# Fourier and attention encoder in fp32: Silu through Tanh, attention scores in two single banks, a one-tensor maxima step, p scaled on VectorE, and the weights' first piece first

## The chip, the cores and the metric

The kernel runs on one core of a Trainium2 chip. The metric is the device time of one execution in microseconds (us); the time before is the median of three runs. All products are fp32 values split into two fp32r parts (high and low), each product being three matmuls (high x high, high x low, low x high).

## The reference

Two sequences, a prompt of 1024 tokens and a sample of 512, go through the same two layers of width 1024. Layer 0 mixes by a Fourier transform, layer 1 by grouped-query attention (8 heads of 128, 2 key/value heads, RMS-normed and rotated q and k). A SwiGLU block of width 2816 follows each.

```python
def run_trunk(x):
    cos, sin = axial_rope_tables(x.shape[1])
    for i in range(DEPTH):                       # DEPTH = 2
        j = i // 2
        if i % 2 == 0:
            x = x + fourier_mixer(x, norm_mix[i], fourier_w[j])
        else:
            x = x + attention_mixer(x, norm_mix[i], attn_w_qkv[j], attn_q_norm[j],
                                    attn_k_norm[j], attn_w_o[j], cos, sin)
        x = x + swiglu_ffn(x, norm_ffn[i], ffn_w_gate[i], ffn_w_up[i], ffn_w_down[i])
    return x

# attention, per block of 128 queries
sc = jnp.einsum('bqkgd,bskd->bkgqs', qi, k).astype(jnp.float32) * scale
p = jax.nn.softmax(sc, axis=-1).astype(v.dtype)
return jnp.einsum('bkgqs,bskd->bqkgd', p, v)

# swiglu
h = rms_norm(x, g)
return (jax.nn.silu(h @ w_gate) * (h @ w_up)) @ w_down
```

## The kernel before

Tokens stand in three blocks of 512: block 0 is the sample, blocks 1 and 2 are the prompt. The program is a set of Python generators that emit instructions; a weaving loop lets two of them take turns by hand-given costs, F ("front": sample) and X ("aux": prompt), each with its own tiles (names that end in F or X) and PSUM banks. A scheduler then orders each engine's instructions by emission order and by when its own model takes them to be ready; an instruction that is `pinned` keeps its place among the pinned ones. On the chip each engine runs its list in order.

PSUM has 8 banks of 128x512 fp32. F has two of tag gF and two of cF, X two of cX and one pair of tag gX (`bank2`, one tile of two banks). `side` and `sides` give one or two working banks.

The order of the work: (1) the sample's Fourier mixer. `turned_weights` reads the folded Fourier weights in 8 pieces of 0.5 MB (`load`); `operand` forms their sum on VectorE (L648) and difference on GpSimd (L649) and splits them (ScalarE L651, GpSimd L652); `product` multiplies them with a DFT matrix; its last part needs `w64`, made from `stage` by `stacked`. `mixer` meanwhile folds the rows (`prepared`, L424 to L427), scales them and multiplies with the token DFT matrix `mat_s`; `mixer_projection` multiplies both. The functions `lead` and `follow` interleave the two. (2) The sample's first SwiGLU (`ffn`) woven with the prompt's Fourier mixer. (3) The prompt's first SwiGLU (`ffn_pair`, a Strassen-like scheme). (4) At its end the sample's q, k, v and attention (`attend` with one block, 32 chunks of 128 queries). (5) The prompt's q, k, v and attention (`attend` with two blocks, 64 chunks), woven with the sample's output projection and second SwiGLU. (6) The prompt's second SwiGLU.

In `attend`, for each chunk `scores` makes the 128 queries' scores against 512 or 1024 keys, takes the maximum of each half (L1371), joins them and scales by the negative factor of the row (L1372), takes Exp with the sum on the side (L1375), the sum's reciprocal (L1376), and multiplies p by it (L1377). `turned` transposes p on TensorE (L1389) and splits it (L242 on ScalarE, L243 on VectorE); `values` multiplies with v. The transposes of a chunk are emitted one chunk behind its scores.

In `ffn` each of 22 slices makes gate and up (24 matmuls each), scales gate by the row's factor (L851), takes Silu on ScalarE (L852), multiplies by the factor again on GpSimd (L853) and with up on VectorE (L854), and splits the result. `here` is true for the sample in layer 0.

Three lines use functions that need a table on ScalarE: L852, L1152 (Silu in `ffn_pair`) and L1375 (Exp). The table loads stand in the trace as ACT_TABLE_LOAD under these lines.

## Time and profile before

| | |
|---|---|
| time before, median of 3 runs | 2921.47 us (2921.27 to 2924.79) |
| the profiled execution | 2916.32 us, span 2914.5 us |
| granted TensorE clock, mean | 0.996 |
| busy share of the span | PE 97%, VectorE 59%, GpSimd 54%, ScalarE 45% |
| DMA moved | 490.53 MB, 168 GB/s on average |

Engines in the profile: PE is TensorE's matmuls and PEld its weight loads, which overlap; DVE is VectorE, ACT ScalarE, POOL GpSimd, SP the engine that issues most DMAs. A row of a group reads: line, engine, operation, out<-in, shapes, count | busy us, mean ns of one | idle time of the engine before them, and what ended it. A row of the timeline reads: start, length, engine, line, operation, names, [idle before it <- what ended that]. A row of the waits reads: who waited <- for whom: us in total, times, longest. A row of a source line gives min/median/max in ns, first and last start in us.

### The profile page before, as it was taken

The page shows a single profiled execution, that of the slowest core. Times are in us where ns is not written, and L with a number is a line of the kernel's source. Part 1 is how long each engine was busy: PE and PEld are TensorE (multiplying, and loading weights), DVE is VectorE, ACT ScalarE, POOL GpSimd, SP SyncE. Part 2 cuts the span into 40 slices and gives each one's busy share as a digit, 9 for nine tenths or more (in the row PEclk, how much of TensorE's full clock was granted, in tenths as well). Part 3 has the DMA queues.
Part 4 walks back from the last instruction along what each step waited for, and adds up shares of the span by engine and source line. Part 5 has one row for each costly group of instructions (what it writes and reads, how often), then busy time and mean ns, then how long its engine had stood idle before and what let it go on. Part 6 is the DMA issues. An engine that isn't in the chain of part 4 may idle for free.

```text
span 2914.5 us, 37209 instructions
## 1 busy us (share of the span) xinstructions
PE 2834.5 (97%) x13656; PEld 2341.5 (80%) x13656; DVE 1714.5 (59%) x3023; ACT 1304.7 (45%) x2134; POOL 1573.4 (54%) x976
## 2 busy tenths in 40 slices
PE   7999999999999999999999999999999999999999
PEld 6778878888888887787778888888888788888887
DVE  6664562466666666847656565553345466666666
ACT  6543242333333333646757776763333333333332
POOL 4445375767776676432332123224637667766774
PEclk9999999999999999999999999999999999999999
DMA  7435474766556653732332112115448865566553
GB/s 233 143 113 179 139 285 174 287 210 227 195 178 215 219 188 112 238 93 92 94 102 84 34 63 71 55 55 184 159 151 303 326 237 195 179 215 221 195 174 116
DMA packets 178870, 490.53 MB, mean 168 GB/s; under 512 B 19488, under 2 KB 29728, under 8 KB 177280
## 3 DMA queue, kind: packets, MB, share of 16 engines
q1 hardware_dynamic: 177760, 483.36, 48.7%
q0 software_dynamic: 640, 3.74, 0.4%
q8 instruction: 108, 1.77, 0.3%
q10 hardware_dynamic: 288, 1.05, 0.1%
q14 instruction: 74, 0.61, 0.1%
HBM read 422.01 MB, written 66.06 MB: 167 GB/s over the span
## 4 chain that ended last, share of the span: by engine, by line
PE 44%; DVE 3%; issue 2%; ACT 1%; DMA 1%; POOL 1%; SPq 0%; POOLq 0%; DVEq 0%; ACTq 0%
PE a L249 6%; PE a L251 6%; PE a L250 6%; PE c L249 5%; PE c L250 5%; PE c L251 5%; PE g L251 3%; PE g L249 3%; PE g L250 3%; PE c L1389 2%; DVE col L1372 1%; DVE col L1371 1%; DVE acc L1074 1%; POOL w L288 0%; ACT p L1375 0%
## 5 line engine op out<-in xcount | busy, mean ns | idle before, releaser
L288 POOL TENSOR_TENSOR w<-raw,w 128x1024 fp32r<-128x1024 f32 x200 | 479.6, 2404 | 762.3 <-ACT w L287 713.8
L243 POOL TENSOR_TENSOR w<-raw,w 128x512 fp32r<-128x512 f32 (+1 forms) x464 | 608.7, 1332 | 443.6 <-ACT w L242 431.6
L242 ACT CAST w<-raw 128x512 fp32r<-128x512 f32 (+1 forms) x464 | 279.5, 632 | 541.1 <-PE a L251 179.7
L287 ACT CAST w<-raw 128x1024 fp32r<-128x1024 f32 x200 | 209.4, 1049 | 275.2 <-PE g L251 94.5
L249 PE MATMUL g<-h,w 128*128 128x512 f32 x704 | 279.0, 396 | 3.5 <-DVE ss L339 2.0
L249 PE MATMUL a<-ring,w 128*128 128x512 f32 x708 | 277.4, 392 | 0.0
L251 PE MATMUL g<-h,w 128*128 128x512 f32 x704 | 276.2, 392 | 0.0
L250 PE MATMUL g<-h,w 128*128 128x512 f32 x704 | 276.1, 392 | 0.0
L251 PE MATMUL a<-ring,w 128*128 128x512 f32 x708 | 275.9, 390 | 0.0
L250 PE MATMUL a<-ring,w 128*128 128x512 f32 x708 | 275.7, 389 | 0.0
L1074 DVE TENSOR_TENSOR acc<-g,acc 128x512 f32<-128x512 f32 x294 | 201.8, 687 | 105.1 <-PE g L251 104.9
L1074 DVE TENSOR_TENSOR acc<-c,acc 128x512 f32<-128x512 f32 x294 | 201.7, 686 | 92.8 <-PE c L251 91.2
L249 PE MATMUL c<-mid,w 128*128 128x512 f32 x604 | 237.0, 392 | 7.0 <-DVE acc L780 4.9
L250 PE MATMUL c<-mid,w 128*128 128x512 f32 x604 | 236.4, 391 | 4.8 <-DVE mid L243 4.8
L251 PE MATMUL c<-mid,w 128*128 128x512 f32 x604 | 236.1, 391 | 0.0
L249 PE MATMUL c<-h,w 128*128 128x512 f32 x480 | 190.5, 398 | 2.1 <-ACT h L245 1.6
L250 PE MATMUL c<-h,w 128*128 128x512 f32 x480 | 188.7, 395 | 0.4 <-DVE h L246 0.2
L251 PE MATMUL c<-h,w 128*128 128x512 f32 x480 | 188.2, 393 | 0.0
L780 DVE TENSOR_TENSOR acc<-c,acc 128x512 f32<-128x512 f32 x176 | 121.0, 688 | 112.7 <-PE c L251 111.8
L249 PEld LDWEIGHTS a<-ring,w 128*128 128x128 f32 x708 | 133.0, 188 | 32.1 <-DVE mid L243 4.3
L249 PEld LDWEIGHTS g<-h,w 128*128 128x128 f32 x704 | 132.5, 188 | 30.1 <-DVE ss L339 2.2
L251 PEld LDWEIGHTS a<-ring,w 128*128 128x128 f32 x708 | 133.1, 188 | 27.9
(393 smaller groups left out, 6727.5 us busy)
## 6 DMA issues: line engine op xcount, KB each, us to landing
ring<-mov_B SPq DMA_DIRECT2D x248, 512.0 KB, 5.5
ring<-mov_T SPq DMA_DIRECT2D x88, 512.0 KB, 5.2
raw<-in_gate_dram SPq DMA_DIRECT2D x44, 512.0 KB, 3.6
raw<-in_up_dram SPq DMA_DIRECT2D x44, 512.0 KB, 3.5
raw<-in_down_dram SPq DMA_DIRECT2D x88, 256.0 KB, 3.0
raw<-in_gate_dram SPq DMA_DIRECT2D x88, 256.0 KB, 5.1
raw<-in_up_dram SPq DMA_DIRECT2D x88, 256.0 KB, 5.3
raw<-in_down_dram SPq DMA_DIRECT2D x44, 512.0 KB, 4.3
```

The source lines that it names most:

```text
L242: keep(act.copy(hi, src))
L243: keep(eng.tensor_tensor(lo, src, hi.bitcast(F32), op=ALU.subtract))
L249: pe.matmul(out, lh, rh, start=first, stop=False, **kw)
L250: pe.matmul(out, lh, rl, start=False, stop=False, **kw)
L251: pe.matmul(out, ll, rh, start=False, stop=last, **kw)
L287: pinned(act.copy(flat[:, 0], raw)) if early else act.copy(flat[:, 0], raw)
L288: pool.tensor_tensor(flat[:, 1], raw, flat[:, 0].bitcast(F32), op=ALU.subtract)
L780: dve.tensor_tensor(acc[dc], box[0], acc[dc], op=ALU.add)
L1074: dve.tensor_tensor(acc, chain[d], acc, op=ALU.add)
L1371: dve.tensor_reduce(st[:, 2 * kb : 2 * kb + 1], sc[:, kb], op=ALU.max, axis=AX.X)
L1372: dve.scalar_tensor_tensor(st[:, 1:2], st[:, 2 * nb - 2 : 2 * nb - 1], st[:, 0:1], nrqc[:, gq, h : h + 1], op0=ALU.max, op1=ALU.mult)
L1389: pe.transpose(tr[:, i * P : (i + 1) * P], p[:, kc * P : (kc + 1) * P], ident)
```

## The change

Six edits in one:

- `ffn` takes Tanh of half the gate instead of Silu, except for the sample in layer 0 (`here`): a new VectorE step forms (tanh + 1) x gate, and the missing half goes into the product with up.
- From the prompt's attention on, X has two single banks of tag gH in place of the pair gX: scores use one bank for each half, `side` and `sides` one each.
- Exp of the prompt's scores is taken in two halves of 512 with two sums, which VectorE adds; p is multiplied by the reciprocal on VectorE (`tensor_scalar`), in the sample still on ScalarE.
- The maxima step is a `tensor_scalar` with two per-partition scalars instead of a `scalar_tensor_tensor`.
- The statistics of a chunk (`st`, `sm`) both have 3 columns and so share one ring of four tiles.
- At the start the first weight piece is loaded ahead of the rows; piece 1, the mask, the stage rows, the token DFT matrix and its row come later; pieces are made one or two steps earlier in `lead`.

```diff
+        "gF": 2, "gX": 1, "gH": 2, "cF": 2, "cX": 2,
...
+    def single():
+        return tl("a", [TB], F32, "gH", pools["psX"])
+
     def side():
-        return bankg() if cur[0] == "F" else bank2()[:, 0]
+        return bankg() if cur[0] == "F" else single() if apart else bank2()[:, 0]
     def sides():
         if cur[0] == "F":
             return [bankg(), bankg()]
+        if apart:
+            return [single(), single()]
...
         load(0)
+        yield
         load(1)
         yield
...
-            act.activation(s, ga, AF.Silu)
+            if here:
+                act.activation(s, ga, AF.Silu)
+            else:
+                act.activation(s, ga, AF.Tanh, scale=0.5)
+                dve.scalar_tensor_tensor(s, s, 1.0, ga, op0=ALU.add, op1=ALU.mult)
             pool.tensor_tensor(s, s, first["r"], op=ALU.mult)
-            dve.tensor_tensor(up, up, s, op=ALU.mult)
+            if here:
+                dve.tensor_tensor(up, up, s, op=ALU.mult)
+            else:
+                dve.scalar_tensor_tensor(up, up, 0.5, s, op0=ALU.mult, op1=ALU.mult)
...
-                    sc = bankg().unsqueeze(1) if nb == 1 else bank2()
+                    sc = [bankg()] if nb == 1 else sides()
...
-                    dve.scalar_tensor_tensor(st[:, 1:2], st[:, 2 * nb - 2 : 2 * nb - 1], st[:, 0:1], nrqc[:, gq, h : h + 1], op0=ALU.max, op1=ALU.mult)
-                    sm = col(2)
+                    dve.tensor_scalar(st[:, 1:2], st[:, 2 * nb - 2 : 2 * nb - 1], st[:, 0:1], nrqc[:, gq, h : h + 1], op0=ALU.max, op1=ALU.mult)
+                    sm = col(3)
                     p = tmp(T) if nb == 1 else tl("p", [T], F32, "pX", ap)
-                    act.activation(p, s_in, AF.Exp, bias=st[:, 1:2], scale=rqc[:, gq, h : h + 1], accum_out=sm[:, 0:1])
+                    for kb in range(nb):
+                        act.activation(p[:, kb * TB : (kb + 1) * TB], sc[kb], AF.Exp, bias=st[:, 1:2], scale=rqc[:, gq, h : h + 1], accum_out=sm[:, 2 * kb : 2 * kb + 1])
+                    if nb == 2:
+                        dve.tensor_scalar(sm[:, 0:1], sm[:, 0:1], sm[:, 2:3], None, op0=ALU.add)
                     dve.reciprocal(sm[:, 1:2], sm[:, 0:1])
-                    act.activation(p, p, AF.Copy, scale=sm[:, 1:2])
+                    if nb == 1:
+                        act.activation(p, p, AF.Copy, scale=sm[:, 1:2])
+                    else:
+                        dve.tensor_scalar(p, p, sm[:, 1:2], None, op0=ALU.mult)
...
+    ws = turned_weights(w64, dd, odd, alt)
+    next(ws)
+    load_rows("s")
...
     def lead():
         next(ws)
+        sp.dma_start(mask, t["mask"])
+        next(ws)
+        pool.dma_start(m_s.rearrange("p c h n -> p (c h n)"), t["dft_s"])
         sp.dma_start(stage[0:96], t["wf64"])
+        row_in("s")
+        rows_of_dft("s")
         m = mixer("s", got_s, u_s, xrs_s, zz_s)
         for k, v in enumerate(m):
             yield v
-            if k == 3:
+            if k == 1:
                 stacked(w64[0:96], stage[0:96], 64)
-            if k < 3 or k % 2 == 0 and k < 14:
+            if k < 2 or k % 2 == 0 and k < 14:
                 next(ws)
...
     open_pool("psX", **RIGHT, **PS)
+    apart.append(True)
```

## The prediction

> **What bounds the kernel now.** I read the page first, then busy time by stage, then what TensorE waits for inside the stages that are not full, then the instructions ahead of those waits.

> ```profile
> span 2914.5 us, 37209 instructions
> PE 2834.5 (97%) x13656; PEld 2341.5 (80%) x13656; DVE 1714.5 (59%) x3023; ACT 1304.7 (45%) x2134; POOL 1573.4 (54%) x976
> ...
> 0.00:19.00 19.00, 14.24 (x87) 13.36 (x88) 8.47 (x15) 10.12 (x19) 6.73 (x13) 1.00 0.82 285
> 19.00:41.00 22.00, 11.62 (x35) 7.38 (x35) 18.97 (x36) 11.22 (x19) 12.75 (x7) 0.69 0.53 170
> 1340.00:1525.00 185.00, 173.41 (x947) 141.70 (x946) 114.02 (x263) 126.49 (x235) 55.38 (x29) 1.00 0.29 90
> 1525.00:1985.00 460.00, 441.17 (x2518) 372.51 (x2517) 277.93 (x507) 322.38 (x459) 130.51 (x60) 1.00 0.19 62
> ```

> The four stage rows give window, length, busy time of PE, PEld, DVE, ACT and POOL, granted clock, DMA share and GB/s. TensorE is the bound: it is busy 2834.5 of 2914.5 us, so 80 us are left. The change takes no matmul of the computation away, so it can only win idle time, and the changed lines touch three places that have some: the start (15.1 us idle to 41 us, part of what counts as busy there being the 72 warm-up matmuls), the sample's attention (1340 to 1525 us, 11.6 idle) and the prompt's (1525 to 1985 us, 18.8 idle).

> What TensorE waits for, first in the sample's window, then in the prompt's (sum, times, longest):

> ```profile
> PE c L1389 <- DVE h L243: 2.0, 3, 1.2
> PE c L249 <- ACT w L242: 1.5, 3, 1.2
> PE c L1389 <- ACT t L1377: 1.4, 1, 1.4
> PE g L249 <- ACT t L1375: 1.3, 2, 0.9
> ...
> PE a L249 <- ACT p L1375: 7.2, 7, 2.1
> PE c L1389 <- ACT p L1377: 5.0, 5, 1.5
> PE c L1389 <- ACT t L1403: 2.1, 2, 1.3
> PE c L1389 <- DVE h L243: 1.4, 1, 1.4
> ```

> These name the last link only. One chain in order of time shows where they begin:

> ```profile
> 1859.02 2.39 POOL L243 TENSOR_TENSOR w<-raw,w 128x1024 fp32r<-128x1024 f32 x1 [5.01 <-ACT w L242]
> 1859.22 2.21 DVE L1372 SCALAR_TENSOR_TENSOR col<-col,nrqc 128x1 f32<-128x1 f32 x1
> 1861.46 1.21 ACT L1375 ACTIVATE p<-a,col,rqc 128x1024 f32<-128x1024 f32 x1 [1.54 <-DVE col L1372]
> 1864.79 0.44 PE L1389 MATMUL c<-ident,p 128*128 128x128 f32 x2 [1.47 <-ACT p L1377]
> ...
> L1372 DVE SCALAR_TENSOR_TENSOR col<-col,nrqc x96: 199/218/2407, 1342.3 to 1976.3; 128x1 f32<-128x1 f32 x96
> L1372 DVE SCALAR_TENSOR_TENSOR col<-col,nrqc 128x1 f32<-128x1 f32 x64 | 41.8, 653 | 0.8
> ```

> A step on 128x1 numbers takes 0.22 us at the median but 2.41 at worst. Here it ends at 1861.43, when POOL's pass ends (1861.41), Exp waits 1.54 us for it, and 3.3 us on TensorE stands 1.47 us. The last row is the group in the prompt's window: 64 of them average 653 ns, so 28 us of VectorE time there are such waits.

> **The maxima step (L1372)** reads two SBUF tensors; it becomes a form with one tensor and two per-partition scalars. Whether that form also waits for POOL is shown by these:

> ```profile
> 26.45 1.59 POOL L649 TENSOR_TENSOR f<-raw 128x512 f32<-128x512 f32 x1
> 26.84 1.22 DVE L436 TENSOR_TENSOR m<-r_s,mask 128x1 f32<-128x1 f32 x1
> 28.13 2.60 POOL L652 TENSOR_TENSOR wm<-f,wm 128x1024 fp32r<-128x1024 f32 x1
> 28.45 0.13 DVE L437 TENSOR_SCALAR m<-m 128x1 f32<-128x1 f32 x1
> 1527.11 2.39 DVE L1323 TENSOR_SCALAR nrqc<-col 128x32 f32<-128x32 f32 x1
> ```

> The two-tensor 128x1 step waited for POOL's end at 28.04; the one-tensor 128x1 step took 0.13 us inside a POOL pass; the one-tensor step on 32 elements took 2.39 us. So the new form escapes at one element (one such row) and not at 32. [...]

> Sample's attention: its multiply stays on ScalarE, so here the wait simply goes. The four quoted rows hold 6.2 us; bounds 0 and 6.2. I take 4, as some of them have no long step ahead.

> **Prompt's scores in two single banks, p multiplied on VectorE.** For each of 64 chunks:

> ```profile
> L1375 ACT ACTIVATE p<-a,col,rqc 128x1024 f32<-128x1024 f32 x64 | 77.4, 1209 | 49.5 <-DVE col L1372 49.2
> L1377 ACT ACTIVATE p<-p,col 128x1024 f32<-128x1024 f32 x64 | 74.0, 1156 | 6.4 <-DVE col L1376 6.4
> L1375 ACT ACTIVATE t<-g,col,rqc 128x512 f32<-128x512 f32 x32 | 24.9, 779 | 17.2 <-DVE col L1372 17.2
> L1375 ACT ACTIVATION_READ_ACCUMULATOR p<-a,col,rqc 128x1 f32 x64 | 12.3, 192 | 0.0
> L1371 DVE TENSOR_REDUCE col<-a 128x1 f32<-128x512 f32 x128 | 82.9, 685 | 71.8 <-PE a L251 71.2
> L537 DVE TENSOR_SCALAR t<-x,r_s 1x512 f32<-1x512 f32 x1 | 0.5, 469 | 0.0
> L243 DVE TENSOR_TENSOR w<-a,w 128x1024 fp32r<-128x1024 f32 x4 | 4.9, 1220 | 1.4 <-ACT w L242 1.4
> ```

> ScalarE: two Exp of 779 + 192 replace one of 1209 + 192, +541 ns; the multiply's 1156 goes. Net -615, times 64 = -39 us. VectorE gains an add of two columns (0.13, L437's kind) and the multiply. A one-tensor step in SBUF takes 0.13 us at 1 and 0.469 at 512 elements, 0.66 ns an element, so 0.81 at 1024; bounds 0.47 (half the elements) and 1.22 (the two-tensor row of the same size). I take 0.80, the nearest form. [...]

> That multiply is over 32 elements, so it must wait for POOL as L1323 did. POOL is busy 130.5 of 460 us in this stage, 28%, mostly in 2.4 us passes: an estimate of 0.28 x 1.2 = 0.34 us a chunk against the 0.44 that L1372 loses now (653 less 210). So three quarters of the wait remains, but behind Exp rather than ahead of it. Bank release then no longer depends on it: the first bank is free after max, maxima step and one Exp, and the second maximum can follow its own matmuls alone. Of the 7.2 us of "a <- p L1375" I take 6 as gone. The other rows (5.0, 2.1, 1.4; 8.5 together) sit behind p or behind VectorE's queue, where the multiply now waits with the transposes' splits, the next maxima and FFN's accumulator adds queued behind it, and behind those TensorE for PSUM banks. The chain from the last score matmul to p gets shorter by 0.68 (first maximum beside the second half's matmuls), 0.36 (1.156 less 0.80) and 0.10 (0.44 less 0.34), longer by 0.54 (second Exp) and 0.13 (add): 0.47 shorter in all. Five waits of 1.0 on average, each 0.47 shorter, and the same share of the rest: I take 4 of 8.5. Together -10; bounds -16 (all 15.7 of the four rows) and, with VectorE overloaded, +17 (rival c). The statistics' tiles now share one ring of four instead of two rings: two chunks deep, and with one chunk of lag between scores and transposes the tile that is reused was last read a whole chunk (some 7 us, 460 over 64) before: nothing.

> **Silu by Tanh, layer 1 of the sample.**

> ```profile
> L852 ACT ACT_TABLE_LOAD x13 | 16.7, 1283 | 0.2
> L1375 ACT ACT_TABLE_LOAD x12 | 15.4, 1283 | 0.2
> L246 DVE SCALAR_TENSOR_TENSOR h<-a,gains,h 128x512 fp32r<-128x512 f32 x16 | 12.0, 747 | 5.1 <-ACT h L245 4.9
> 2256.18 1.29 POOL L853 TENSOR_TENSOR t<-t,ss 128x512 f32<-128x512 f32 x1
> 2259.10 0.70 DVE L854 TENSOR_TENSOR g<-g,t 128x512 f32<-128x512 f32 x1 [5.48 <-PE g L251]
> ```

> 22 times VectorE gets a 0.75 us step (L246's kind) between Tanh and POOL's product; the last product changes form at the same price within 0.05. Even where FFN runs alone POOL's product was done 1.6 us before "up" ended (2257.47 against 2259.10), and L854 waited for TensorE, so 0.75 is covered; without that cover it would be 22 x 0.75 = 16.5. The new step waits on VectorE for Tanh (some 0.78, the Exp row of that size), and what is queued behind it there waits too; in the prompt's stage that is 11 times and VectorE has 40% to spare. Of 25 table loads 22 go if Tanh needs none after Exp: 28.2 us of ScalarE's 322 in the prompt's stage and after. No row shows Tanh's table; the bounds are 0 and 28.2 of ScalarE time, and both are worth nothing by themselves, since ScalarE is 70% busy and the waits above begin at L1372. A later ffn_pair then loads Silu once, 1.28, beside matmuls. [...] FFN: 0.

> **Weights' first piece first.**

> ```profile
> 11.98 0.69 DVE L424 TENSOR_TENSOR x<-c,x 128x512 f32<-128x512 f32 x1 [2.03 <-DMA x<-in_rows_s_dram]
> 14.59 1.28 POOL L649 TENSOR_TENSOR f<-raw 128x512 f32<-128x512 f32 x1 [10.67 <-DMA raw<-in_wf_dram]
> 30.89 0.34 PEld L249 LDWEIGHTS c<-mat_s,comb 128*128 128x128 f32 x1
> ```

> On SP piece 0 goes ahead of the rows (one issue, some 0.6 us), piece 1, mask and stage after them; ScalarE's two row issues stay. On POOL the 1 MB DFT matrix and its row move behind the first piece's two passes (1.3 + 2.6), and so behind their waits for piece 0 and for ScalarE's split of it; the eo constants come first. DMA runs at 0.82 to 19 us, so order decides: 0.5 MB come before the rows, 1 MB after. The matrix is wanted at 30.9; from some 12 us on it has time. VectorE is the busiest to 41 us (18.97 of 22): it may lose the 2.03 us wait for rows and do piece 0's sum (0.7, a two-tensor step like L424) before them. Piece 2's sum and the split of the stage rows move ahead of the root that scales the rows and stood behind it: the same VectorE work in another order. Products of the weights go out earlier, which fills TensorE's cold stretch (clock 0.69), but the stretch ends when VectorE has the rows' units ready. So I take the two VectorE terms, 2.03 + 0.7, as -3; bounds -10 (piece 0 is first used at 14.59 now; if all follows it forward, at most the 10.4 us that TensorE idles from 19 to 41) and +2 (rows later by an issue and 0.5 MB at 285 GB/s).

> **Sum:** -4 - 10 - 3 = -17 on the profiled run's 2916.3 (span 2914.5 plus 1.8) is 2899.3. The median of the runs is 5.2 higher, so 2904.5.

> **Rivals.** (a) The wait only moves: VectorE's queue and p are as late as today and the prompt wins nothing: -4 - 3 = -7, 2914.5. For it: POOL's 2.4 us passes and L1323's 2.39; against: Exp and the banks no longer stand behind it. (b) One element waits too: then L1372 goes on as now, and the multiply waits besides. Nothing is won in the sample; in the prompt 3 of the 7.2, since a bank comes free 0.43 (1.209 less 0.779) sooner in each of seven waits; start -3: -6, 2915.5. [...] For it: the 32-element step; against: the 0.13 us row. (c) Slower: VectorE becomes the prompt's bound. Its 277.9 of 460 us take 64 x (1.22 + 0.34 + 0.14) = 109 and 11 x 0.75 = 8, less 28: 367, 80%, and each multiply holds back a split that frees a PSUM bank. If TensorE's waits there double (+17), -7 + 17 = +10, 2931.5; it decides from 13 us of new waits on, 0.2 a chunk. Against: at 0.80 the share is 74%.

> **Numbers.** Forecast 0.60, (a) 0.16, (b) 0.10, (c) 0.14. A change under 0.2%, 5.8 us, can't be told from none. (a) and (b) lie on that line, half of each on either side: faster 0.60 + 0.13, same 0.13, slower 0.14. The range goes from 2892 (-29, of the lower bounds' -6 - 15.7 - 10) to 2919 (-2: the start's +2 and a quarter of the 14 in the attentions), which takes in the forecast, (a) and (b) and leaves out (c) and the tails.

> **What would show it.** Right: L1372 at 0.2 us throughout; no "a <- Exp" wait over 0.5 us; the multiply 0.8 at the median and up to 3 us when POOL runs; no table loads from 1620 to 2015; POOL's first pass (L649) at about 7 us instead of 14.59. Wrong: L1372 still up to 2.4; TensorE waiting over 10 us for p after 1525; idle time to 41 us over 15.

## The result, and the profile after

The changed kernel takes 2902.41 us (median of four, 2899.95 to 2902.70) against 2921.37 us (2918.89 to 2924.79): a ratio of 0.9932, 95% interval 0.992 to 0.9945, so 19 us faster. One of the twelve runs of e2 below took 4723.8 us at a granted clock of 0.555 and is left out of e2's row. Lines have moved: the maxima step is L1384 (before L1372), Exp L1388 (L1375), the sum's add L1390 (new), the reciprocal L1391 (L1376), the prompt's multiply L1395 (on VectorE), the sample's L1393 (L1377, on ScalarE), the transposes L1407 (L1389); L243 and L249 to L251 are L248 and L254 to L256; L649, L302 and L424 are L655, L307 and L429.

The changed kernel's totals on the page, then its busy time by stage (columns as in the prediction):

```profile
span 2900.9 us, 37485 instructions
PE 2844.9 (98%) x13656; PEld 2348.8 (81%) x13656; DVE 1765.6 (61%) x3173; ACT 1226.6 (42%) x2176; POOL 1574.7 (54%) x976
```

```profile
0.00:19.00 19.00, 14.10 (x91) 12.74 (x91) 8.63 (x14) 10.57 (x20) 8.30 (x13) 1.00 0.90 302
19.00:41.00 22.00, 12.22 (x34) 7.62 (x35) 21.14 (x38) 13.79 (x24) 15.75 (x8) 0.84 0.56 168
1340.00:1525.00 185.00, 177.93 (x972) 146.87 (x971) 107.85 (x278) 128.01 (x239) 56.28 (x29) 0.99 0.30 95
1525.00:1985.00 460.00, 453.70 (x2585) 386.77 (x2584) 324.81 (x653) 249.69 (x507) 138.90 (x63) 1.00 0.22 71
```

TensorE's idle time fell from 11.6 to 7.1 us in the sample's attention and from 18.8 to 6.3 us in the prompt's, 17 us together. To 41 us it stayed: 15.1 before, 14.7 now.

What TensorE waits for in the prompt's window now (sum, times, longest); before, this list began with 7.2 us for Exp's bank:

```profile
PE c L1407 <- DVE p L1395: 3.2, 4, 1.6
PE a L256 <- POOL w L248: 1.7, 1, 1.7
PE c L254 <- DVE pt L248: 1.0, 1, 1.0
PE c L1407 <- DVE pt L248: 0.3, 1, 0.3
```

The changed instructions, by line (durations in ns: least, median, most), and then their groups in the prompt's window and all that is left of the table loads:

```profile
L1384 DVE TENSOR_SCALAR col<-col,nrqc x96: 253/272/277, 1348.1 to 1964.7; 128x1 f32<-128x1 f32 x96
L1395 DVE TENSOR_SCALAR p<-p,col x64: 742/753/2843, 1535.5 to 1967.5; 128x1024 f32<-128x1024 f32 x64
```

```profile
L1395 DVE TENSOR_SCALAR p<-p,col 128x1024 f32<-128x1024 f32 x64 | 50.7, 792 | 1.6
L1390 DVE TENSOR_SCALAR col<-col 128x1 f32<-128x1 f32 x64 | 13.6, 213 | 50.4 <-ACT p L1388 50.2
L862 DVE SCALAR_TENSOR_TENSOR t<-t,g 128x512 f32<-128x512 f32 x11 | 7.5, 682 | 1.2 <-ACT t L861 1.1
```

```profile
L225 ACT ACT_TABLE_LOAD x1 | 1.3, 1283 | 1.2 <-PEq L1719 1.2
L859 ACT ACT_TABLE_LOAD x1 | 1.3, 1283 | 0.0
L1388 ACT ACT_TABLE_LOAD x1 | 1.3, 1283 | 0.0
L1165 ACT ACT_TABLE_LOAD x1 | 1.3, 1283 | 0.0
```

The maxima step never waits now: 96 times, at most 277 ns, where 2407 was seen before. 33 of the 96 lie wholly inside a pass on POOL. Of the two-tensor steps before none does: 31 took over 300 ns, and each of them ended 11 to 23 ns behind an instruction of POOL. The multiply costs 0.75 us, and 0.79 with its waits. Each of the four loads left is the only one of its line, so the 22 Tanh (L861) between the Exps took none.

### The profile page after: what moved, and what is told of

Its sections match the earlier page's. It is cut to its first block, busy times and chain, and to the rows that moved or that the text cites. A ratio compares the mean times of both kernels' runs of the same rounds, so it can differ in the third digit from the quotient of the medians.

```text
span 2900.9 us, 37485 instructions
## 1 busy us (share of the span) xinstructions
PE 2844.9 (98%) x13656; PEld 2348.8 (81%) x13656; DVE 1765.6 (61%) x3173; ACT 1226.6 (42%) x2176; POOL 1574.7 (54%) x976
## 4 chain that ended last, share of the span: by engine, by line
PE 85%; DVE 6%; ACT 2%; issue 2%; DMA 2%; POOL 2%; SPq 0%; ACTq 0%; POOLq 0%; DVEq 0%
PE a L254 11%; PE a L256 11%; PE a L255 11%; PE c L254 10%; PE c L255 9%; PE c L256 9%; PE g L254 7%; PE g L256 7%; PE g L255 7%; PE c L1407 2%; POOL w L293 1%; DMA raw<-in_up_dram 1%; DVE acc L1087 1%; PE c L1272 1%; ACT w L292 1%
## 5 line engine op out<-in xcount | busy, mean ns | idle before, releaser
L248 POOL TENSOR_TENSOR w<-raw,w 128x512 fp32r<-128x512 f32 (+1 forms) x464 | 608.1, 1331 | 432.7 <-ACT w L247 409.6
L254 PE MATMUL g<-h,w 128*128 128x512 f32 x704 | 280.1, 398 | 3.5 <-DVE ss L344 1.8
L254 PE MATMUL a<-ring,w 128*128 128x512 f32 x708 | 277.3, 392 | 0.0
L256 PE MATMUL g<-h,w 128*128 128x512 f32 x704 | 277.1, 394 | 0.0
L256 PE MATMUL a<-ring,w 128*128 128x512 f32 x708 | 276.0, 390 | 0.0
L254 PE MATMUL c<-mid,w 128*128 128x512 f32 x604 | 237.2, 393 | 4.7 <-DVE acc L786 2.4
L256 PE MATMUL c<-mid,w 128*128 128x512 f32 x604 | 235.9, 391 | 0.0
L254 PE MATMUL c<-h,w 128*128 128x512 f32 x480 | 192.1, 402 | 2.0 <-ACT h L250 1.6
L256 PE MATMUL c<-h,w 128*128 128x512 f32 x480 | 190.4, 398 | 0.0
L254 PEld LDWEIGHTS a<-ring,w 128*128 128x128 f32 x708 | 132.9, 188 | 32.1 <-DVE mid L248 4.3
L254 PEld LDWEIGHTS g<-h,w 128*128 128x128 f32 x704 | 132.9, 189 | 30.3 <-DVE ss L344 2.0
L256 PEld LDWEIGHTS a<-ring,w 128*128 128x128 f32 x708 | 132.9, 188 | 28.0
```

The source lines that it names most:

```text
L248: keep(eng.tensor_tensor(lo, src, hi.bitcast(F32), op=ALU.subtract))
L254: pe.matmul(out, lh, rh, start=first, stop=False, **kw)
L256: pe.matmul(out, ll, rh, start=False, stop=last, **kw)
```

## The experiments

All times, each with the ratio to runs of the kernel before on the same chip. Kernels of a block were run together; a ratio can be compared across blocks, a median only roughly.

| kernel | us | ratio | 95% interval |
|---|---|---|---|
| changed kernel | 2902.4 | 0.9932 | 0.9920 to 0.9945 |
| e1: changed, old start | 2901.1 | 0.9941 | 0.9925 to 0.9956 |
| e2: before + new start | 2922.2 | 1.0009 | 0.9997 to 1.0020 |
| e3: before + one-tensor step | 2893.6 | 0.9913 | 0.9896 to 0.9929 |
| e4: changed, two-tensor step | 2921.6 | 1.0010 | 1.0000 to 1.0020 |
| e5: changed, p on ScalarE | 2897.6 | 0.9921 | 0.9907 to 0.9936 |
| e6: changed, pair of banks | 2906.7 | 0.9947 | 0.9932 to 0.9962 |
| e7: changed, Silu | 2905.4 | 0.9945 | 0.9931 to 0.9958 |
| e8: e3 without the two-column ring | 2907.4 | 0.9954 | 0.9941 to 0.9968 |
| f1: changed + 128 unused bytes | 2894.2 | 0.9912 | 0.9895 to 0.9929 |
| f2: e5 + 128 unused bytes | 2890.2 | 0.9899 | 0.9879 to 0.9918 |
| f3: e3 + 128 unused bytes | 2901.6 | 0.9943 | 0.9926 to 0.9960 |
| f4: e3 + 256 unused bytes | 2894.7 | 0.9912 | 0.9894 to 0.9931 |

### First block: which part carries the gain

**e3, the step alone** in the kernel before:

```
- dve.scalar_tensor_tensor(st[:, 1:2], st[:, 2*nb-2 : 2*nb-1], st[:, 0:1], nrqc[...], op0=ALU.max, op1=ALU.mult)
+ dve.tensor_scalar(st[:, 1:2], st[:, 2*nb-2 : 2*nb-1], st[:, 0:1], nrqc[...], op0=ALU.max, op1=ALU.mult)
```

> The kernel before with the one-tensor maxima step alone; banks, Exp, p's multiply on ScalarE and Silu as before. Theory 'wait for POOL': the step's 40 us of waits vanish (0.2 us at the median, none over 0.5) and with them most of TensorE's waits behind them, 5 in the sample's attention and 10 to 14 of 16 in the prompt's: 2921.4 - 15 to -19 = 2902 to 2906, as much as the whole change. Theory 'chain and banks': the step is a small part, -4 to -6, 2916, and the rest comes from the halves, the banks and ScalarE's load.

One line gives 0.9913, about 25 us, more than the whole change and more than the 15 to 19 us of the theory. Its step, the prompt's stage, and all that TensorE still waits for there, from three views:

```profile
L1372 DVE TENSOR_SCALAR col<-col,nrqc x96: 255/266/276, 1342.8 to 1952.1; 128x1 f32<-128x1 f32 x96
```

```profile
1525.00:1985.00 460.00, 459.11 (x2626) 391.52 (x2625) 253.48 (x506) 327.01 (x467) 137.66 (x63) 1.00 0.22 75
```

```profile
PE c L249 <- DVE pt L243: 0.5, 1, 0.5
PE c L1389 <- ACT p L1377: 0.2, 1, 0.2
```

TensorE idles 0.9 of 460 us, against 18.8 before and 6.3 in the whole change. The waits for banks ("a <- p") are gone and those for p ("c <- p") fell from 5.0 to 0.2 us, although banks, Exp and the multiply are as before: they began at this step.

**e4, all but the step**: the line above turned back in the changed kernel.

> The changed kernel with the old two-tensor maxima step. 'Wait for POOL': the step waits again in about a third of its 96 runs, up to 2.4 us, ahead of Exp, and the time goes up by 10 to 16, to 2912 to 2918. 'Chain and banks': the shorter chain and the single banks cover most of it, +3 to +5, 2906.

1.0010, slower than either theory had it: without the step, the rest wins nothing (a cost that was found later, that of the addresses, is inside this number). TensorE's idle time in the prompt's stage is 15.6 us, against 18.8 before. The longest of the prompt's waits of e4 show where the time stays:

```profile
PE c L254 <- DVE pt L248: 4.6, 7, 1.1
PE a L254 <- ACT p L1388: 2.8, 3, 1.7
PE a L256 <- POOL w L248: 2.5, 1, 2.5
PE c L1407 <- DVE pt L248: 2.1, 3, 1.6
PE c L1407 <- DVE col L1384: 1.5, 1, 1.5
```

The bank's wait fell from 7.2 to 2.8 us, as single banks were to bring. By these rows, what stands behind the stalled step on VectorE (the transposes' splits, pt) became late in its place; no run takes the two apart.

**e1 and e2, the start**: undone in the changed kernel (e1), and done alone in the kernel before (e2; shortened here, e1 is the reverse).

```
- load_rows("s"); pool.dma_start(m_s, t["dft_s"]); row_in("s"); sp.dma_start(mask, ...)
+ next(ws)                       # the weights' first piece
+ load_rows("s")
+ ... next(ws); sp.dma_start(mask, ...); next(ws); pool.dma_start(m_s, t["dft_s"]) ...
```

> The changed kernel with the start in its old order; everything from the sample's first SwiGLU on as changed. Theory 'start costs': the new start puts TensorE at the same place by 90 us as the old one and then meets a stretch of half clock from 92.4 us on for 10.2 us, so without it the time is some 3.5 us shorter than the changed kernel's 2902.4, 2899, and the trace shows no half clock between 41 and 130 us. Theory 'start gains', as predicted: 3 us longer, 2905.5. If the half clock at 92 us is chance of one execution, within 1 us of 2902.4.

> The kernel before with the new start alone. 'Start costs': 3.5 us longer than before's 2921.4, 2925, with half clock near 92 us. 'Start gains': 2918.4. The root that scales the sample's rows ends near 32 us instead of 25.4 by either, since this was seen in the changed kernel.

1.0009 alone and 0.9941 against 0.9932 when undone: nothing that can be measured, in either direction. The half-clock stretch on which the theory of a cost rested (10.2 us from 92.4 us on) is in e2's profile too, and e1 has one of 3.4 us at 83.4 us, yet neither time shows a cost. The order of time (start in us, duration) shows why. Of the kernel before, the prediction has POOL's first pass at 14.59 and the first load from mat_s at 30.89; the rows' first step on VectorE and their root, of the same kernel, are:

```profile
8.67 1.29 DVE L424 TENSOR_TENSOR x<-c,x 128x512 f32<-128x512 f32 x2 [7.67 <-DMA x<-in_rows_s_dram]
...
25.44 0.16 DVE L302 SCALAR_TENSOR_TENSOR r_s<-c,col 128x4 f32<-128x4 f32 x1
```

The same four in the changed kernel:

```profile
8.82 1.77 POOL L655 TENSOR_TENSOR f<-raw 128x512 f32<-128x512 f32 x1 [5.98 <-DMA raw<-in_wf_dram]
...
11.22 1.92 DVE L429 TENSOR_TENSOR x<-c,x 128x512 f32<-128x512 f32 x3 [1.76 <-DMA x<-in_rows_s_dram]
...
32.38 0.15 DVE L307 SCALAR_TENSOR_TENSOR r_s<-c,col 128x4 f32<-128x4 f32 x1
...
36.60 0.29 PEld L254 LDWEIGHTS c<-mat_s,comb 128*128 128x128 f32 x1 [0.37 <-ACT comb L247]
```

The weights come 5.8 us earlier, and the rows pay for it: their first step is 2.6 us later, the root 6.9, the first DFT product 5.7. The two orders trade one wait for the other.

### Second block: what takes a part of the step's gain back

The whole change holds the step and is still 9 us above e3 by the medians (0.9932 against 0.9913). Four suspects, each by itself.

**e5, p multiplied on ScalarE again**:

```
- if nb == 1: act.activation(p, p, AF.Copy, scale=sm[:, 1:2])
- else:       dve.tensor_scalar(p, p, sm[:, 1:2], None, op0=ALU.mult)
+ act.activation(p, p, AF.Copy, scale=sm[:, 1:2])
```

> The changed kernel with one edit undone: the prompt's p is multiplied by the sum's reciprocal on ScalarE again, as the kernel before does. The changed kernel alone is 2902.4 us; the maxima step alone gives 2893.6. Theory: the multiply on VectorE is what takes back a part of the step's gain (64 x 0.79 us more on VectorE in 1525-1985 us, and TensorE's waits for p on VectorE, 3.2 us in four); without it the time falls by about 5 us, to some 2897, and the waits of the transposes for p on VectorE are gone. Rival, the prediction's: the multiply unloads ScalarE and helps or costs nothing; then 2902 to 2906, with waits for p on ScalarE in their place.

2897.6 us, near the theory's 2897, though the intervals of e5 and of the changed kernel overlap. Its prompt's waits:

```profile
PE a L254 <- ACT p L1388: 1.7, 1, 1.7
PE a L256 <- POOL w L248: 1.4, 1, 1.4
PE c L1404 <- DVE pt L248: 0.5, 1, 0.5
PE c L1404 <- ACT p L1392: 0.5, 1, 0.5
```

The wait for p is 0.5 us in place of 3.2, while one wait for a bank, 1.7, is new. TensorE's idle time in the stage is 4.2 us in place of 6.3.

**e6, the pair of banks and one Exp of 1024**:

```
- for kb in range(nb): act.activation(p[...], sc[kb], AF.Exp, ..., accum_out=sm[:, 2*kb : 2*kb+1])
- if nb == 2: dve.tensor_scalar(sm[:, 0:1], sm[:, 0:1], sm[:, 2:3], None, op0=ALU.add)
+ act.activation(p, s_in, AF.Exp, ..., accum_out=sm[:, 0:1])       # s_in: both banks
```

> The changed kernel with one edit undone: the prompt's scores go into the pair of banks again and one Exp reads all 1024 columns, in place of two single banks and two Exps with an add of their sums; p stays on VectorE. Theory: with the step no longer waiting, the halves are an extra 64 Exps' fixed cost and an extra add for each chunk and nothing else; without them the time falls by about 3 us, to some 2899. Rival, the prediction's: the single banks come free earlier and are worth a part of the 10 us of the prompt's stage; then the waits of the scores for a bank that Exp reads return, 3 to 5 us, and the time is about 2906.

2906.7, the rival's number; the theory that the halves cost 3 us falls. That the single banks win anything is not shown: the intervals of e6 and of the changed kernel overlap. The bank's wait comes back, smaller than the 7.2 us of before, now that the step no longer stalls:

```profile
PE a L254 <- ACT p L1389: 2.6, 3, 2.2
PE a L256 <- POOL w L248: 1.7, 1, 1.7
```

The wait for p shrinks beside it (0.3 us, from 3.2), and TensorE's idle time in the stage is 5.8 us, against 6.3 in the changed kernel.

**e7, Silu**: the Tanh, its VectorE step and the 0.5 of the last product go, `act.activation(s, ga, AF.Silu)` returns.

> The changed kernel with Silu as its own function again in place of Tanh and VectorE's step for it. Theory: 22 table loads of 1.28 us return on ScalarE and VectorE loses its steps of 0.68 us for them; both stand beside TensorE's matmuls, so the time stays within 1 us of 2902.4. Rivals: the loads stand in the way of an Exp or of a Silu that TensorE waits for, then +2 us or more; or VectorE's step is what costs in the SwiGLU stages, then -2 us, and the matmuls' mean spacing in 700-1000 us falls from 228.6 to 227.7 ns.

2905.4: 3 us above the changed kernel, and intervals that overlap. TensorE idles 8.9 us in the prompt's stage in place of 6.3. Tanh is worth 0 to 3 us; that its VectorE step costs in the other stages is ruled out, as e7's matmuls still follow each other at 228.6 ns in the mean (the next experiments show what that hangs on).

**e8, the addresses alone**, e3 with `sm = col(3)` for `sm = col(2)`. The changed kernel takes the sums from the ring of three-column tiles. The ring of two-column tiles, four of 32 bytes a partition, then no longer exists, and every tile laid out behind it lies 128 bytes lower. Tiles laid out from the other end, such as op, stay.

> The kernel before with the one-tensor maxima step (2893.6 us by itself) and one more edit: the sum's column is taken from the ring of three-column tiles, as the changed kernel takes it, so that the ring of two-column tiles is gone and the tiles allocated after it lie at other addresses. No instruction is added or moved. Theory: the changed kernel's slower matmuls in the SwiGLU stages (mean spacing 228.6 against 227.7 ns in 700-1000 us) come from these addresses; then the spacing is 228.6 here too and the time is about 4 us longer, 2897.5. Rival: they come from something else that the change does; then the spacing is 227.7 ns and the time within 1 us of 2893.6.

0.9954 against e3's 0.9913, with not one instruction added: some 12 us, three times what the theory asked for. This is the cost that no part of the prediction had.

### Third block: the addresses

```
+ cols.tile([P, 32], F32, tag="pad", name="pad", bufs=1)     # 128 bytes; 256 in f4; never used
```

> The changed kernel (2902.4 us) with 128 unused bytes a partition allocated in the pool of columns, so that the tiles behind it lie at the addresses of the kernel before. No instruction differs. Theory: the lost ring of two-column tiles is the whole of what takes the step's gain back (0.41% between the step alone with and without the ring), so the time falls by 10 to 14 us, to 2889 to 2893, and the matmuls' mean spacing in 700-1000 us is 227.7 ns again. Rival: only the spacing's part, some 7 us, comes back, and the rest between the two kernels was the clock at the start; then about 2896. Second rival: the addresses matter only together with the old order of work; then 2901 to 2904.

> The kernel before with the one-tensor maxima step (0.9913 of before) and 128 unused bytes a partition, so that the tiles behind it lie 128 bytes higher. No instruction differs. Theory: what counts is where these tiles lie modulo 256 bytes against those that are laid out from the other end, which do not move; then 128 up is as bad as 128 down: 0.995 of before, spacing 228.6 ns. Rival: moving them down did harm by something particular to those addresses; then 0.9913 and 227.7 ns.

> The same with 256 bytes. Theory (modulo 256): as the kernel with the step alone, 0.9913 of before, spacing 227.7 ns. Rival: any other place than the old one costs, 0.995 and 228.6 ns.

f1 got 8 us back by the medians and 6 by the ratios, a little under the theory's 10 to 14 and between it and the first rival; the second rival falls. It stands where e3 stands (0.9912 and 0.9913): at the old addresses the other five edits together win and lose nothing that these intervals, 5 us to either side, could show. In the profiles they take and give: TensorE idles 6.7 us in f1's prompt's stage and 0.9 in e3's, but 0.6 and 5.0 from 1985 to 2400 us. f3 and f4 differ as their theory had it. The stage from 500 to 1000 us, where TensorE is full in all kernels and the work is the same; rows in the order e3, e8, the changed kernel, f1, f3, f4:

```profile
500.00:1000.00 500.00, 499.00 (x2196) 409.90 (x2195) 307.90 (x481) 180.08 (x321) 354.95 (x246) 1.00 0.62 213
```

```profile
500.00:1000.00 500.00, 498.99 (x2188) 408.35 (x2187) 306.81 (x478) 180.33 (x321) 354.01 (x245) 1.00 0.62 211
```

```profile
500.00:1000.00 500.00, 499.02 (x2188) 408.43 (x2187) 306.25 (x479) 181.10 (x323) 354.35 (x245) 1.00 0.62 212
```

```profile
500.00:1000.00 500.00, 499.01 (x2196) 409.90 (x2195) 306.77 (x479) 181.55 (x323) 355.61 (x247) 1.00 0.61 212
```

```profile
500.00:1000.00 500.00, 498.96 (x2188) 408.34 (x2187) 305.67 (x477) 179.56 (x320) 354.13 (x245) 1.00 0.61 210
```

```profile
500.00:1000.00 500.00, 498.97 (x2195) 409.86 (x2194) 306.97 (x480) 180.00 (x321) 356.63 (x247) 1.00 0.62 213
```

With the tiles at the old place (e3, f1) or 256 bytes up (f4), 2195 or 2196 matmuls start in 500 us; 128 bytes down (e8, the changed kernel) or up (f3), 2188. TensorE is as busy and waits for next to nothing in both (1 us of 500); each matmul is 0.36% slower on average. The distance from one start to the next tells how: from 700 to 1000 us its mean is 227.7 to 227.8 ns in the one group and 228.6 to 228.7 in the other, the median 227 in both, the 95th percentile 227 to 229 in the one and 235 in the other. About one in ten takes 5 to 8 ns more. The groups that read op, from 700 to 1000 us, are among them (e3, then e8):

```profile
L251 PE MATMUL a<-op,w 128*128 128x512 f32 x40 | 15.6, 389 | 0.0
```

```profile
L251 PE MATMUL a<-op,w 128*128 128x512 f32 x40 | 15.8, 394 | 0.0
```

So the place modulo 256 bytes fits all four places that were tried, and both rivals of f3 and f4 fall. Four pairs price it: 0.41% (e8 to e3), 0.31% (f3 to f4), 0.20% (changed to f1) and 0.22% (e5 to f2), 6 to 12 us. That two blocks of tiles must agree, and not the one block by itself, fits that op did not move and its matmuls became slower. The addresses that the built kernels give their tiles bear it out, with the starts of the same matmuls compared one by one (those of 512 columns, 222 to 246 ns apart). In e3 and f1 the streamed operand and the weights that are loaded for the next matmul lie in the same half of a 256-byte step in all but one of these cases. In e8 they lie in different halves in 1540 cases, and there the distance to the next start is 4.3 ns longer than in e3 in the mean; in the 8157 others it is 0.5 longer. In the changed kernel against f1 it is 4.1 ns (1578 cases) and 0.5 (8204).

**f2, the best version**: e5 with the 128 bytes.

> The same 128 bytes in the changed kernel whose prompt's p is multiplied on ScalarE (0.9921 of before, about 5 us better than the changed kernel). Theory: the two gains add, as they lie in different things (waits for p, addresses): 5 us below the padded changed kernel, some 2885 to 2888, the best version. Rival: with the matmuls at full rate the waits for p fall elsewhere and the multiply's place is worth nothing; then within 2 us of the padded changed kernel.

0.9899, 2890.2 us, the lowest of all, 2 us above what was expected. The multiply's place is worth 0.13% beside f1, as it was 0.11% without the bytes: two pairs that agree, each inside its own interval.

## Why the prediction was right, and where its steps were not

The forecast was 2904.5 and the time is 2902.4. The sum came out for the mechanism that it named first, but its terms share the gain out wrongly, and that the total is so near is in part luck: costs that it did not have and gains that it did not have nearly cancel (the last two paragraphs of this section).

**The step: right.** One element with one tensor does not wait for POOL, in 192 cases of two kernels (253 to 277 ns), 65 of them wholly inside a POOL pass. Rival (b), by which one element waits too, fell with it.

**The sample's -4: right** (11.6 less 7.1 is 4.5 us of idle time).

**The prompt's -10: size near, cause wrong.** 12.5 us of idle time went. The prediction gave that to the single banks and the shorter chain, and left the step only what lay ahead of Exp. The failed step is "three quarters of the wait remains, but behind Exp rather than ahead of it". It took the multiply to meet a POOL pass as often as chance would have it, 0.34 us a chunk. Measured: a mean of 792 ns against a median of 753, 0.04 a chunk; three of 64 waited, the longest for the 2843 ns in the row of L1395 above. In eight other cases POOL's pass began 0.11 to 0.54 us behind the multiply's start and took 2.46 to 2.90 us, against 2.40; this is one of them:

```profile
1741.99 0.76 DVE L1395 TENSOR_SCALAR p<-p,col 128x1024 f32<-128x1024 f32 x1
1742.10 2.90 POOL L248 TENSOR_TENSOR w<-raw,w 128x1024 fp32r<-128x1024 f32 x1 [1.04 <-ACT w L247]
```

With the stall gone at its root, e3 shows that nothing was left in this stage for the other edits to win: idle time 0.9 us. Without it, the other edits take the 18.8 us only to 15.6 (e4). So the gain here belongs to the step.

**Rival (c), VectorE as the bound: false as a bound, true in small.** VectorE is busy 324.8 of 460 us, 71%, near the 74% worked out. Still TensorE waits 3.2 us for p on VectorE, and moving the multiply there seems to lose 3 to 5 us (e5, f2; each pair inside its interval), where the prediction had it shorten the chain. Its 0.80 us was right (0.75); the queue on VectorE was priced too low, behind accumulator adds and splits of 0.68 each. **Rival (a)** fell: the waits did not move, they went.

**Tanh's 0: right** within what can be told (0 to 3 us), with the 22 table loads gone and 0.68 us for the new VectorE step where 0.75 was taken.

**The start's -3: wrong.** It measured nothing. The step that failed is "the same VectorE work in another order", together with taking two VectorE terms as saved: the order put the weights' steps ahead of the root, and root and first DFT product came 6.9 and 5.7 us later. The sign named for it, POOL's pass at about 7 us, came nearly (8.8), and was no sign of a gain. The bound that was named for harm, an issue and 0.5 MB on the rows' way, was the right place: the rows' first step came 2.6 us later.

**Two things it did not have.** The shared ring was priced "nothing", by the reuse of its tiles; what it did was to move addresses, +6 to +12 us. And a gap of the kernel before outside the changed stages is gone:

```profile
2264.09 1.08 DVE L1035 TENSOR_TENSOR s<-raw,raw 128x512 f32<-128x512 f32 x1 [4.29 <-DMA raw<-in_gate_dram]
2265.10 0.68 DVE L243 TENSOR_TENSOR mid<-g,mid 128x512 fp32r<-128x512 f32 x1
...
2265.83 0.79 PE L250 MATMUL c<-mid,w 128*128 128x512 f32 x1 [4.08 <-DVE mid L243]
```

There VectorE waits for weights with the split that TensorE needs queued behind. e3, e8, f3 and f4 still have it, 4.1 us. In e2, with the new start alone, it is 1.8 us, and in the changed kernel and in e1 (without the new start), e4, e5, e6 and e7 TensorE waits at most 2.1 us for anything there. So the start shortens it by itself, and the other edits do without the start; which of them is open.

On the profiled executions the terms are: attentions -17.0, idle time from 1985 to 2400 us -4.5 (5.1 to 0.6), slower matmuls +10.5 (8 x 0.228 in 500 us, by 2900, an estimate; compared one by one, the changed kernel's full-rate distances are 11.0 us longer in sum than f1's), start about 0: -11, against -13.6 measured. That is near, but it leaves out the clock. TensorE's busy time in its half-clock stretches, by half, is an estimate of what they cost: 7.2 us before and 14.1 after, +6.9. With it, and with all of TensorE's idle time (80.0 to 56.0 us, -24.0), the sum is -6.6, and 7 us stay open. Waits too short to show as idle time, between matmuls whose records are 389 ns long and start every 227, could be these; no run shows it for the changed kernel (e3, whose clock cost as much as before's, is busy 2830.5 us against 2834.5 with the same matmuls).

Two errors of the forecast met at its end: the profiled run came 3.4 us above the 2899.3 worked out for it, and the 5.2 us between profiled run and median, which the prediction carried over, was not there after (2902.68 against 2902.41). The three lower bounds from which its range starts add up to -31.7, not -29; nothing hangs on it.

## What to carry to other kernels

When several waits of different names lie downstream of one stalled instruction, mend that instruction alone first: here one line won 25 us, and the five edits around it added nothing to that. An edit that drops or adds a small ring moves every tile allocated behind it; restore the old addresses with unused bytes before judging the edit, or its own worth is mixed with theirs. Work that starts earlier at the start of a kernel is a gain only if the chain that ends the stretch does not stand behind it.

## What the runs showed of the hardware

The spread among runs of one kernel goes with the granted clock in most kernels: e2's go from 2914.1 us at 0.996 to 2926.7 at 0.992; e7's five, from 2903.3 at 0.994 to 2906.9 at 0.995, do not show it. In the profiles TensorE drops to half its clock for stretches of 3.4 us and their multiples (3.41 us at 1620.6 and 2265.8 us in the kernel before, 10.24 at 92.4 in the changed one). In all 14 profiles, each stretch between 60 us and the last matmul begins behind 3.4 us in which TensorE had idled for 1.1 to 3.4 us, and they stand behind the same few waits: the 4.1 us at 2262 us in the kernel before has one behind it, and so has the same wait in e3, e8, f3 and f4. A shorter wait has one in some executions and not in others (the 2.2 us for L317 or L322 in the sample's attention: none before, one after), and the same start can run at different clocks: from 19 to 41 us the new one shows 0.60 in e5 and 0.84 in e7. A difference of a few microseconds between two profiled executions in one stage is no evidence until that column has been read.
